# Fewer dense columns, wider gathered rows and another order of picking in a two-tile expert layer

## Chip, cores and metric

One NeuronCore of a Trainium2 chip runs the whole program. The metric is the device time of one launch in microseconds. "PE" is the matrix engine, "DVE" the vector engine, "ACT" the scalar engine, "POOL" the GpSimd engine, "SP" the engine that only issues transfers here.

## What is computed

The program is one encoder block for 256 tokens of 2,048 columns: a combined projection, a gated linear attention, a differential attention, an output projection, and then the part that this change touches, a layer of 16,384 single-neuron experts. Cut to that part, the reference is:

```python
qb = (xb @ w_q).reshape(TB, 8, 2, 128)
s = einsum('thpc,hpnc->thpn', qb, sub_keys)
sv, si = top_k(s, 16)                      # per head: 16 of 128, twice
cand = sv[..., 0, :, None] + sv[..., 1, None, :]
cv, ci = top_k(cand.reshape(..., 256), 16) # 16 experts of 16384
g = softmax(cv)
u, vv = u_tab[eidx], v_tab[eidx]           # rows of 2048 columns
a = gelu(einsum('thkd,td->thk', u, xb))
out = einsum('thk,thkd->td', g * a, vv)
```

Each token has 8 heads of 16 experts, so 128 "slots". A slot needs the dot product of one row of `peer_u` with the token, and later a weighted row of `peer_v`.

## The kernel before

The 256 tokens are two tiles of 128, tile 0 and tile 1. The first expert layer (the dot products) is split by columns of `peer_u`.

**Dense part.** The first `DU = KU*128 = 896` columns are multiplied for all 16,384 experts. A host-side transposed copy `c_uT` comes in as 128 blocks of 128 experts. A block is a tile `ur` (L916, loaded at L917 on SP's queue, `NU = 3` buffers) and seven products per block (L919) with the 256 tokens moving; an f32 product is two instructions in the trace. ACT copies the results (L921) into `Y = [W0, W1]`, two tiles of 64 KB per partition, indexed by expert row and column.

**Gathered part.** The other 1,152 columns are fetched row by row: for each slot `gather_dot` issues an indirect transfer on POOL's queue (L761) of one row for each of 128 tokens into a buffer `g` (`NG = 5` buffers), and DVE forms the dot product with `xb` (L765) into `dots`. There are 128 such gathers for each tile. Before them DVE routes each head (`route`, L731 to L757: top 16 twice, indices, softmax numerator).

**Picking.** When all dense results stand, `pick(tt, t4)` takes those of the chosen experts for four tokens: it loads the row indices broadcast to all partitions (`ib`, L782, three buffers), spreads the column indices by PE (L786), makes a one-hot matrix on ACT (L788, L789), multiplies `Y` with it on PE (L792), selects the row on DVE (L793), sums over partitions on PE (L795) and scales on DVE (L797). There are 32 picks for a tile. `slots_of` (L768 to L777) prepares the indices of a tile, by PE transposes (L773), after its routing.

**Weights.** `weights_of(tt, sT)` adds gathered and dense parts, applies Gelu and the softmax weights, and leaves a row of slot weights in `sT[:, 2]`. `build_w` then writes, four tokens at a time, the weights into a dense expert matrix, W0 for tile 0 and W1 for tile 1: two one-hot matrices (`oj` by POOL, ACT and DVE in turn, `oi` by DVE at L901) and a product (L903). W0 is built in place of tile 0's dense results while tile 1 is picked, and W1 after `weights_of(1)`. Then the second expert layer runs in the same two-part manner (from L985) to the end.

**Order.** The order of instructions on each engine is fixed when the program is built, by a list scheduler with its own estimate of durations: it takes the earliest instruction of the program text that it thinks ready. In the text, all of tile 0's gathers and tile 1's routing come first, then the dense products, then tile 1's gathers with picks and W0 builds between those of heads `H0 = 3` to 7. Each engine runs its instructions in the fixed order, and waits at an instruction whose inputs are not there.

Of the kernel before, what the change touches and what calls it, by code (L numbers as in the profile page):

```python
# [10 lines left out]
F32 = mybir.dt.float32  # L11
# [4 lines left out]
AF = mybir.ActivationFunctionType  # L16
ALU = mybir.AluOpType
# [3 lines left out]
P = 128  # L21
# [19 lines left out]
def block_kernel(ctx: ExitStack, tc: tile.TileContext, A: dict, out: bass.AP):  # L41
    nc = tc.nc
# [11 lines left out]
    bt = pool("bt")  # L54
# [18 lines left out]
    def pa(shape):  # L73
        return paux.tile(list(shape), F32, tag="pa", name="pa")
# [15 lines left out]
    iota = cc[:, 128:256]  # L90
    onec = cc[:, 256:257]
# [61 lines left out]
    for k in range(KT):  # L153
        ps = pa([P, N])
# [488 lines left out]

    KU = 7
    DU = KU * P
    rgt = ExitStack()
    rp = pool("rp", side="right", c=rgt)
# [7 lines left out]

    hgd = rp.tile([P, KU, T], F32, name="hgd")
    hg = [None] * KT
    gf = vrow["g_ffn"]  # L660
    w_o = A["c_w_out"]
    for j in range(8):
# [10 lines left out]
        for b in range(2):  # L673
# [3 lines left out]
            for tt in range(2):  # L677
                nc.tensor.transpose(p2[:, tt * P:(tt + 1) * P], hs[:, tt, k * P:(k + 1) * P], ident)
            hg[k] = hgd[:, k] if k < KU else s2p.tile([P, T], F32, tag=f"s2_{k}", name=f"hg{k}")
            nc.scalar.activation(hg[k], p2, AF.Copy, scale=g)  # L680
# [31 lines left out]
    dots = [gwt[:, tt, 1, :] for tt in range(2)]  # L712
    gsum = [gst[:, tt, :] for tt in range(2)]
    u_tab = A["peer_u"][0]
    NG = 5
    NU = 3
    NI = 3

    def top16(vo, io, src, n):
# [47 lines left out]

    def slots_of(tt):  # L768

        r = bt.tile([P, 3, P], F32, tag=f"b{2 + tt}", name=f"slotT{tt}")  # L770
        ps = pa([P, 2, P])
        for a in range(2):
            nc.tensor.transpose(ps[:, a, :], ij[tt][:, a, :], ident)  # L773
        nc.scalar.activation(r[:, 0:2], ps, AF.Copy)
        nc.scalar.activation(jr[:, tt], ij[tt][:, 1, :], AF.Copy)
        nc.scalar.dma_start(ijd[tt].rearrange("a (b c) -> (a b) c", b=4), ij[tt][:, 0, :])
        return r  # L777

    def pick(tt, t4):

        ib = ep.tile([P, 4, P], F32, tag="ib", name="ib", bufs=NI)
        nc.sync.dma_start(ib.rearrange("p a b -> p (a b)"), ijd[tt][t4:t4 + 1, :].to_broadcast([P, 4 * P]))  # L782
        pj = pa([P, 4, P])
        for q in range(4):
            t = t4 * 4 + q
            nc.tensor.matmul(pj[:, q, :], lhsT=identr[:, t:t + 1].to_broadcast([P, P]), rhs=jr[:, tt], start=True, stop=True)  # L786
        oj = rp.tile([P, 4, P], F32, tag="ohx", name="ojT", bufs=2)
        nc.scalar.activation(oj, pj, AF.Abs, bias=mrow, scale=1.0)  # L788
        nc.scalar.activation(oj, oj, AF.Relu, bias=onec, scale=-1.0)  # L789
        pz = pm([P, 4, P])  # L790
        for q in range(4):
            nc.tensor.matmul(pz[:, q, :], lhsT=Y[tt][:, :, t4 * 4 + q], rhs=oj[:, q, :], start=True, stop=True)  # L792
        nc.vector.scalar_tensor_tensor(ib, ib, prow, pz, op0=ALU.is_equal, op1=ALU.mult)  # L793
        for q in range(4):
            nc.tensor.matmul(pj[:, 0, q:q + 1], lhsT=ib[:, q, :], rhs=onec, start=True, stop=True)  # L795
        ts = slice(t4 * 4, t4 * 4 + 4)
        nc.vector.tensor_mul(dT[:, tt, ts], pj[:, 0, 0:4], rstb[:, tt, ts])  # L797

    def weights_of(tt, sT):

        rc = rp.tile([P, 8], F32, tag="rcs", name="rcs", bufs=2)
        nc.vector.reciprocal(rc, gsum[tt])
        g3 = gw[tt].rearrange("p (h k) -> p h k", k=16)
        nc.vector.tensor_mul(g3, g3, rc.unsqueeze(2).to_broadcast([P, 8, 16]))
        ps = pa([P, 2, P])
        nc.tensor.transpose(ps[:, 0, :], dots[tt], ident)
        nc.tensor.transpose(ps[:, 1, :], gw[tt], ident)
        nc.vector.tensor_add(dT[:, tt], dT[:, tt], ps[:, 0, :])
        nc.scalar.activation(dT[:, tt], dT[:, tt], AF.Gelu)
        nc.vector.tensor_mul(sT[:, 2], dT[:, tt], ps[:, 1, :])  # L810
        ps = pa([P, P])
        nc.tensor.transpose(ps, sT[:, 2], ident)
        nc.scalar.activation(gw[tt], ps, AF.Copy)
# [6 lines left out]
    def queries(h):  # L820
        qt = bt.tile([P, 2, T], F32, tag=f"b{2 + h % 2}", name="pqt")

        def ev_pq(b, ps):
            with tc.high_priority():
                nc.scalar.activation(qt[:, b, :], ps, AF.Copy)
        ps = [pm((P, T)) for _ in range(2)]
        for kh in range(2):
            for k0, raw in load_raw(w_q, h * 256, kh, wait[h][kh]):
                for kk in range(raw.shape[1]):
                    k = k0 + kk  # L830
                    for b in range(2):
                        nc.tensor.matmul(ps[b], lhsT=raw[:, kk, b * P:(b + 1) * P], rhs=hg[k], start=(k == 0), stop=(k == KT - 1))
        for b in range(2):
            ev_pq(b, ps[b])
        with tc.high_priority():
            for tt in range(2):
                ps = pa([P, 2, P])
                for p in range(2):
                    nc.tensor.matmul(ps[:, p, :], lhsT=qt[:, p, tt * P:(tt + 1) * P], rhs=skT[h // 2][:, 2 * (h % 2) + p, :],
                                     start=True, stop=True)  # L840
                s_ = rp.tile([P, 2, P], F32, tag="sS", name="sS", bufs=3)
                nc.scalar.activation(s_, ps, AF.Copy, scale=rst[tt])
                if tt == 0:
                    s0 = s_
            nc.scalar.dma_start(sS1d[h], s_)
            eis[0, h] = route(0, h, s0)
# [14 lines left out]
    rstb = rp.tile([P, 2, P], F32, name="rstb")  # L861
    for tt in range(2):
        ps = pa([P, P])
        nc.tensor.transpose(ps, rst[tt].to_broadcast([P, P]), ident)
        nc.scalar.activation(rstb[:, tt], ps, AF.Copy)
    ijd = [drp.tile([32, 4 * P], F32, name=f"ijd{tt}") for tt in range(2)]
    dT = rp.tile([P, 2, P], F32, name="dT")
    wpc.close()
    ph0.close()
    ph1.close()  # L870
# [4 lines left out]
    W0 = wp01.tile([P, P, P], F32, name="W0")  # L875
# [3 lines left out]
    W1E = "pav"  # L879


    def build_w(oi4, wt, sT, t4):
        ps = pa([P, 4, P])
        for q2 in range(2):
            oj = bt.tile([P, 2, P], F32, tag="ow", name="oj1", bufs=4)
            t = t4 * 4 + q2 * 2
            m = W1E[(t4 * 2 + q2) % len(W1E)]
            if m == "a":
                for q in range(2):
                    nc.scalar.activation(oj[:, q], iota, AF.Abs, bias=sT[:, 1, t + q:t + q + 1], scale=-1.0)  # L890
                nc.scalar.activation(oj, oj, AF.Relu, bias=onec, scale=-1.0)
            elif m == "p":
                for q in range(2):
                    nc.gpsimd.tensor_scalar(oj[:, q], iota, sT[:, 1, t + q:t + q + 1], None, op0=ALU.is_equal)  # L894
            else:
                nc.vector.tensor_tensor(
                    oj, iota.unsqueeze(1).to_broadcast([P, 2, P]), sT[:, 1, t:t + 2].unsqueeze(2).to_broadcast([P, 2, P]),
                    op=ALU.is_equal)
            for q in range(2):
                oi = oi4[:, q2 * 2 + q]  # L900
                nc.vector.tensor_scalar(oi, iota, sT[:, 0, t + q:t + q + 1], sT[:, 2, t + q:t + q + 1], op0=ALU.is_equal,  # L901
                                        op1=ALU.mult)
                nc.tensor.matmul(ps[:, q2 * 2 + q, :], lhsT=oj[:, q], rhs=oi, start=True, stop=True)  # L903
        nc.scalar.activation(wt[:, :, t4 * 4:t4 * 4 + 4], ps.rearrange("p t i -> p i t"), AF.Copy)

    for h in range(8):
        for k in range(16):
            gather_dot(0, h, k, eis[0, h])
        s_ = rp.tile([P, 2, P], F32, tag="sS", name="sS", bufs=3)
        nc.scalar.dma_start(s_, sS1d[h])  # L910
        eis[1, h] = route(1, h, s_)

    for g in range(P // 2):
        ps = pm([P, 2, T])
# [8 lines left out]
    epc = ExitStack()  # L923
    ep = pool("ep2", side="right", c=epc)
    sTs = [slots_of(tt) for tt in range(2)]
    work = [lambda t4=t4: pick(0, t4) for t4 in range(32)] + [lambda: weights_of(0, sTs[0])]
    for t4 in range(32):
        work.append(lambda t4=t4: pick(1, t4))
        work.append(lambda t4=t4: build_w(ep.tile([P, 4, P], F32, tag="oi4", name="oi4", bufs=2), W0, sTs[0], t4))

    H0 = 3
    done, n = 0, len(work)
    for h in range(8):
        for k in range(16):
# [142 lines left out]
def host_vectors(inputs):  # L1077

    r = {"c_vec": np.concatenate([np.asarray(inputs[nm]).reshape(n, P) for nm, n in VEC])}
    w = np.asarray(inputs["w_in"])[0]  # L1080
    r["c_w_in"] = host_blocks(np.concatenate([w[:, :OFF_LR], w[:, OFF_DQ:]], axis=1), 256)
    r["c_w_lr"] = host_blocks(w[:, OFF_LR:OFF_DQ], 32)[0]
    for nm in ("w_branch_gla", "w_branch_diff", "w_out", "peer_w_q"):
        r["c_" + nm] = host_blocks(np.asarray(inputs[nm])[0], 256)

    r["c_uT"] = np.ascontiguousarray(np.asarray(inputs["peer_u"])[0][:, :7 * P].reshape(P, P, 7, P).transpose(0, 3, 2, 1))
    return r


# [50 lines left out]
```

## Time and profile before

| What | Value |
|---|---|
| median of 3 runs | 2665.92 us (2665.3 to 2668.43) |
| profiled execution, its time | 2668.04 us |
| profiled execution, its span | 2666.2 us |
| mean granted PE clock in it | 0.959 of full speed |
| busy PE / DVE / ACT / POOL | 2511.2 / 1937.0 / 1081.0 / 984.3 us |

The span runs from the first to the last instruction of the trace; 1.8 us of the time lie around it. The expert layer's first half lies between about 1187 us (first gather) and 2090 us of the span.

### The profile page before, as it was taken

What the parts mean: (1) busy time and instruction counts of PE and PEld (TensorE: products, weight loads), DVE (VectorE), ACT (ScalarE), POOL (GpSimd) and SP (SyncE); (2) the same over time, 40 slices, a digit from 0 to 9 for tenths busy, and PEclk for the clock granted to TensorE, in tenths of its full rate; (3) what the DMA queues carried; (4) which work ended last, traced back from release to release, by engine and by line L of the source; (5) the groups of instructions that cost most, each with busy time, mean ns of one, the idle gap of its engine ahead of it and who ended that gap; (6) DMA issues with size and microseconds to landing.
All of it is one profiled execution on the core that took longest, in us unless ns stands there. A gap on an engine that the chain in (4) does not pass through costs nothing.

```text
span 2666.2 us, 43563 instructions
## 1 busy us (share of the span) xinstructions
PE 2511.2 (94%) x16631; PEld 2386.3 (90%) x16631; DVE 1937.0 (73%) x3179; ACT 1081.0 (41%) x1948; POOL 984.3 (37%) x999
## 2 busy tenths in 40 slices
PE   8999999999999999999796999989999999999996
PEld 7999999999999999998675777779998889999996
DVE  4778877557777875439997666652357999899998
ACT  4555554345555544421111000013466544444444
POOL 1333310001011001015655655420013777777776
PEclk9999999999999999999898999985699999999998
DMA  4344445554454564579899999971123588888886
GB/s 161 139 155 163 145 171 185 184 188 153 159 169 165 185 225 135 203 267 369 291 372 347 410 408 408 404 267 64 60 68 118 194 303 306 311 317 313 311 309 238
DMA packets 141470, 622.39 MB, mean 233 GB/s; under 512 B 17906, under 2 KB 22828, under 8 KB 116412
## 3 DMA queue, kind: packets, MB, share of 16 engines
q1 hardware_dynamic: 78960, 382.96, 41.2%
q0 software_dynamic: 59216, 230.04, 23.1%
q10 hardware_dynamic: 3084, 6.59, 0.7%
q8 instruction: 131, 2.15, 0.3%
q14 instruction: 79, 0.65, 0.1%
HBM read 613.07 MB, written 5.37 MB: 232 GB/s over the span
## 4 chain that ended last, share of the span: by engine, by line
PE 55%; DVE 15%; issue 13%; POOL 9%; DMA 7%; ACT 0%; POOLq 0%; DVEq 0%; ACTq 0%
PE pm L205 11%; PE pm L203 11%; PE pm L204 11%; POOL g L761 7%; DMA gv<-in_peer_v_dram,ent 5%; PE pm L792 4%; DVE g L765 3%; DVE hs L970 3%; PE pa L795 3%; PE acc L1008 2%; PE pa L903 2%; DMA g<-in_peer_u_dram,ent 1%; PE acc L1009 1%; PE pa L786 1%; DVE vlo L1002 1%
## 5 line engine op out<-in xcount | busy, mean ns | idle before, releaser
L189 DVE TENSOR_TENSOR lo<-raw,hi 128x1024 fp32r<-128x1024 f32 x352 | 451.2, 1283 | 255.6 <-ACT hi L188 253.8
L205 PE MATMUL pm<-hT,lo 128*128 128x256 f32 (+1 forms) x2048 | 579.0, 286 | 7.9 <-DVE lo L189 7.9
L203 PE MATMUL pm<-hT,hi 128*128 128x256 f32 (+1 forms) x2048 | 583.1, 286 | 0.0
L204 PE MATMUL pm<-hT,hi 128*128 128x256 f32 (+1 forms) x2048 | 582.8, 285 | 0.0
L188 ACT ACTIVATE hi<-raw 128x1024 fp32r<-128x1024 f32 x352 | 372.5, 1059 | 333.0 <-PE pm L204 269.7
L765 DVE SCALAR_TENSOR_TENSOR g<-g,xb 128x1152 f32<-128x1152 f32 x256 | 352.9, 1380 | 139.0 <-DMA g<-in_peer_u_dram,ent 137.9
L919 PE MATMUL pm<-hgd,ur 128*128 128x256 f32 x1792 | 408.4, 385 | 34.7 <-DMA ur<-in_c_uT_dram 31.7
L919 PEld LDWEIGHTS pm<-hgd,ur 128*128 128x128 f32 x1792 | 335.6, 191 | 106.5 <-DMA ur<-in_c_uT_dram 30.6
L205 PEld LDWEIGHTS pm<-hT,lo 128*128 128x128 f32 x2048 | 386.2, 190 | 10.7 <-DVE lo L189 9.0
L203 PEld LDWEIGHTS pm<-hT,hi 128*128 128x128 f32 x2048 | 387.5, 189 | 0.4
L204 PEld LDWEIGHTS pm<-hT,hi 128*128 128x128 f32 x2048 | 387.4, 189 | 0.2
L761 POOL DMA_INDIRECT g<-in_peer_u_dram,ent x256 | 289.2, 1130 | 242.9 <-DVE g L765 170.2
L967 POOL DMA_INDIRECT gv<-in_peer_v_dram,ent x256 | 311.9, 1219 | 131.8 <-DVE hs L970 78.4
L1009 PE MATMUL acc<-vhi,wb 128*128 128x368 f32 x1024 | 329.4, 332 | 0.0
L970 DVE SCALAR_TENSOR_TENSOR hs<-gv,gwt,hs 128x576 f32<-128x576 f32 x256 | 285.6, 1115 | 30.8 <-DMA gv<-in_peer_v_dram,ent 26.9
L1009 PEld LDWEIGHTS acc<-vhi,wb 128*128 128x128 f32 x1024 | 191.8, 189 | 0.0
L1008 PE MATMUL acc<-vlo,wwv 128*128 128x368 f32 x512 | 169.3, 341 | 13.3 <-DVE vlo L1000 7.3
L1008 PE MATMUL acc<-vlo,wb 128*128 128x368 f32 x512 | 169.3, 339 | 10.7 <-DVE vlo L1000 4.0
L921 ACT ACTIVATE W<-pm 128x256 f32<-128x256 f32 x128 | 41.9, 380 | 322.8 <-PE pm L919 321.1
L894 POOL TENSOR_SCALAR oj<-cc,slotT 128x128 f32<-128x128 f32 x88 | 59.1, 683 | 253.8 <-PE pa L903 243.3
L792 PE MATMUL pm<-ojT,W 128*128 128x128 f32 x512 | 127.9, 410 | 0.5 <-ACT W L921 0.5
L1008 PEld LDWEIGHTS acc<-vlo,wwv 128*128 128x128 f32 x512 | 95.9, 189 | 24.9 <-DVE vlo L1000 11.3
(882 smaller groups left out, 4669.2 us busy)
## 6 DMA issues: line engine op xcount, KB each, us to landing
raw<-in_c_w_in_dram SPq DMA_DIRECT2D x128, 1024.0 KB
ur<-in_c_uT_dram SPq DMA_DIRECT2D x128, 448.0 KB
raw<-in_c_w_branch_gla_dram SPq DMA_DIRECT2D x16, 1024.0 KB
raw<-in_c_w_out_dram SPq DMA_DIRECT2D x16, 1024.0 KB
raw<-in_c_w_branch_diff_dram SPq DMA_DIRECT2D x16, 1024.0 KB
ib<-ijd SPq DMA_DIRECT2D x64, 256.0 KB
raw<-in_c_peer_w_q_dram SPq DMA_DIRECT2D x13, 1024.0 KB
g<-in_peer_u_dram,ent POOLq DMA_INDIRECT x256
```

Source lines behind the costliest of these rows:

```text
L188: nc.scalar.activation(hi, src, AF.Copy)
L189: nc.vector.tensor_sub(lo, src, hi.bitcast(F32))
L203: nc.tensor.matmul(ps[b], lhsT=wh, rhs=ah, start=(k == 0), stop=False)
L204: nc.tensor.matmul(ps[b], lhsT=wh, rhs=al, start=False, stop=False)
L205: nc.tensor.matmul(ps[b], lhsT=wl, rhs=ah, start=False, stop=(k == KT - 1))
L761: nc.gpsimd.indirect_dma_start(out=g, out_offset=None, in_=u_tab, in_offset=bass.IndirectOffsetOnAxis(ap=ei[:, k:k + 1], axis=0), element_ ...
L765: nc.vector.scalar_tensor_tensor(g, g, 1.0, xb[:, tt, :], op0=ALU.mult, op1=ALU.mult, accum_out=dots[tt][:, s:s + 1])
L919: nc.tensor.matmul(ps[:, b, :], lhsT=ur[:, k, :], rhs=hgd[:, k, :], start=(k == 0), stop=(k == KU - 1))
L967: nc.gpsimd.indirect_dma_start(out=g, out_offset=None, in_=v_tab, in_offset=bass.IndirectOffsetOnAxis(ap=eis[tt, s // 16][:, s % 16:s % 16 ...
L970: nc.vector.scalar_tensor_tensor(hs[:, tt, DC:], g, gw[tt][:, s:s + 1], hs[:, tt, DC:], op0=ALU.mult, op1=ALU.add)
L1008: nc.tensor.matmul(o, lhsT=wh[:, tt, :], rhs=lo[:, ns], start=False, stop=False)
L1009: nc.tensor.matmul(o, lhsT=wl[:, tt, :], rhs=hi[:, ns], start=False, stop=last(tt))
```

## The change

The dense part shrinks from seven to five blocks of 128 columns (640), so a gathered row grows from 1,152 to 1,408 columns. The U blocks get five buffers of 640 columns instead of three of 896, the row buffers are four instead of five, and the score buffers `sS` two instead of three. The sums `dT` of the dense part move into a fourth slice of the tile `slotT`. In the builds of W0 alone, all `oj` are made by POOL, and every second `oi` by three ACT instructions instead of one of DVE. Picks and W0 builds lie among tile 1's heads 2 to 7 instead of 3 to 7.

```diff
-    KU = 7
+    KU = 5
...
-    NG = 5
-    NU = 3
+    NG = 4
+    NU = 5
...
-        r = bt.tile([P, 3, P], F32, tag=f"b{2 + tt}", name=f"slotT{tt}")
+        r = bt.tile([P, 4, P], F32, tag=f"b{2 + tt}", name=f"slotT{tt}")
...
-        nc.vector.tensor_mul(dT[:, tt, ts], pj[:, 0, 0:4], rstb[:, tt, ts])
+        nc.vector.tensor_mul(dTs[tt][:, ts], pj[:, 0, 0:4], rstb[:, tt, ts])
...
-                s_ = rp.tile([P, 2, P], F32, tag="sS", name="sS", bufs=3)
+                s_ = rp.tile([P, 2, P], F32, tag="sS", name="sS", bufs=2)
...
-            m = W1E[(t4 * 2 + q2) % len(W1E)]
+            m = "p" if wt is W0 else W1E[(t4 * 2 + q2) % len(W1E)]
...
-                nc.vector.tensor_scalar(oi, iota, sT[:, 0, t + q:t + q + 1], sT[:, 2, t + q:t + q + 1], op0=ALU.is_equal,
-                                        op1=ALU.mult)
+                if wt is W0 and q:
+                    nc.scalar.activation(oi, iota, AF.Abs, bias=sT[:, 0, t + q:t + q + 1], scale=-1.0)
+                    nc.scalar.activation(oi, oi, AF.Relu, bias=onec, scale=-1.0)
+                    nc.scalar.activation(oi, oi, AF.Copy, scale=sT[:, 2, t + q:t + q + 1])
+                else:
+                    nc.vector.tensor_scalar(oi, iota, sT[:, 0, t + q:t + q + 1], sT[:, 2, t + q:t + q + 1], op0=ALU.is_equal,
+                                            op1=ALU.mult)
...
+    dTs = [r[:, 3] for r in sTs]
...
-    H0 = 3
+    H0 = 2
```

## Rows read from the trace of the kernel before

**Rows 1.** The page's slices of the span: granted PE clock and transfer rate.

```profile
PEclk9999999999999999999898999985699999999998
...
GB/s 161 139 155 163 145 171 185 184 188 153 159 169 165 185 225 135 203 267 369 291 372 347 410 408 408 404 267 64 60 68 118 194 303 306 311 317 313 311 309 238
```

**Rows 2.** Busy us of each engine (instructions) by stage; last clock, DMA share, GB/s.

```profile
core 0: us, PE busy (x) PEld busy (x) DVE busy (x) ACT busy (x) POOL busy (x), PEclk, DMA share, GB/s
...
1187.00:1285.00 98.00, 92.16 (x439) 81.41 (x438) 83.16 (x243) 11.27 (x34) 53.62 (x55) 0.97 0.89 325
1285.00:1418.00 133.00, 97.68 (x434) 81.69 (x433) 128.97 (x401) 15.89 (x59) 83.22 (x85) 0.91 0.93 341
...
1435.00:1762.00 327.00, 300.08 (x1324) 245.18 (x1322) 208.11 (x305) 30.95 (x94) 176.50 (x153) 1.00 1.02 408
1762.00:1778.00 16.00, 8.70 (x39) 8.25 (x38) 11.77 (x19) 3.48 (x6) 5.47 (x5) 0.83 0.75 274
1778.00:1904.00 126.00, 124.60 (x595) 124.54 (x596) 29.94 (x71) 41.30 (x59) 0.00 (x0) 0.53 0.22 67
1904.00:1938.00 34.00, 34.00 (x216) 34.00 (x216) 18.19 (x56) 21.40 (x44) 6.18 (x10) 0.85 0.16 52
1938.00:2037.50 99.50, 98.52 (x682) 98.25 (x681) 52.95 (x155) 60.59 (x118) 20.30 (x34) 0.98 0.19 61
2037.50:2090.00 52.50, 44.08 (x295) 39.51 (x296) 49.78 (x160) 43.73 (x103) 33.46 (x48) 0.92 0.36 127
```

**Rows 3.** The page's costliest groups: the dense products (busy, mean ns | idle before).

```profile
L919 PE MATMUL pm<-hgd,ur 128*128 128x256 f32 x1792 | 408.4, 385 | 34.7 <-DMA ur<-in_c_uT_dram 31.7
```

**Rows 4.** Groups by line and form, 1285 to 1435 us.

```profile
L761 POOL DMA_INDIRECT g<-in_peer_u_dram,ent x60 | 65.5, 1091 | 52.5 <-DVE g L765 14.9 <-DVE tk L723 8.4 <-DVE si L725 7.7
...
L773 PE MATMUL pa<-cc,ijt 128*128 128x128 f32 x4 | 1.4, 442 | 28.7 <-DVE ijt L750 28.7
```

**Rows 5.** Busy time by stage, the dot products (L765) alone; two instructions each.

```profile
1187.00:1418.00 231.00, 122.94 (x172) 0.93 0.91 335
```

**Rows 6.** Groups by line and form, 1435 to 1762 us.

```profile
L765 DVE SCALAR_TENSOR_TENSOR g<-g,xb 128x1152 f32<-128x1152 f32 x153 | 207.8, 1358 | 119.1 <-DMA g<-in_peer_u_dram,ent 118.9
```

**Rows 7.** Timeline of DVE at 1763 us (start us, us).

```profile
1763.88 1.36 DVE L765 SCALAR_TENSOR_TENSOR g<-g,xb 128x1152 f32<-128x1152 f32 x1
...
1765.27 1.36 DVE L765 SCALAR_TENSOR_TENSOR g<-g,xb 128x1152 f32<-128x1152 f32 x1
```

**Rows 8.** Timeline of PE's weight loads, the same build product at two clocks.

```profile
1917.44 1.83 PEld L903 LDWEIGHTS pa<-oi,oj 128*128 128x128 f32 x8
...
1966.90 0.99 PEld L903 LDWEIGHTS pa<-oi,oj 128*128 128x128 f32 x8
```

**Rows 9.** Groups by line, 1762 to 2037.5 us.

```profile
L793 DVE SCALAR_TENSOR_TENSOR ib<-ib,cc,pm 128x512 f32<-128x512 f32 x64 | 47.7, 747 | 94.4 <-PE pm L792 93.0 <-DMA ib<-ijd 1.4
...
L789 ACT ACTIVATE ojT<-ojT,cc 128x512 f32<-128x512 f32 x62 | 44.7, 720 | 1.8
L788 ACT ACTIVATE ojT<-pa,cc 128x512 f32<-128x512 f32 x62 | 42.3, 682 | 94.3 <-PE pa L786 92.1 <-PE pm L792 2.1
L901 DVE TENSOR_SCALAR oi<-cc,slotT 128x128 f32<-128x128 f32 x128 | 38.1, 353 | 12.3 <-PE pa L903 11.0
...
L894 POOL TENSOR_SCALAR oj<-cc,slotT 128x128 f32<-128x128 f32 x44 | 26.5, 613 | 238.0 <-PE pa L903 227.6 <-DVE dT L797 6.3 <-DVE oj L896 4.0
L904 ACT ACTIVATE W<-pa 128x512 f32<-128x512 f32 x32 | 19.0, 592 | 25.0 <-PE pa L903 25.0
L890 ACT ACTIVATE oj<-cc,slotT 128x128 f32<-128x128 f32 x42 | 14.4, 392 | 13.1 <-PE pa L903 13.1
```

**Rows 10.** Timeline at 1325 us: four `oj` of POOL among dot products of DVE.

```profile
1326.63 3.85 POOL L894 TENSOR_SCALAR oj<-cc,slotT 128x128 f32<-128x128 f32 x4
...
1328.10 1.41 DVE L765 SCALAR_TENSOR_TENSOR g<-g,xb 128x1152 f32<-128x1152 f32 x1
```

**Rows 11.** Timeline of POOL at 1763 us: gathers that wait for nothing shown.

```profile
1763.51 1.11 POOL L761 DMA_INDIRECT g<-in_peer_u_dram,ent  x1 [0.30 <-issue]
```

More of the change, by code (lines that the diff above doesn't have):

```diff
@@ L807, in weights_of @@
         nc.tensor.transpose(ps[:, 1, :], gw[tt], ident)
-        nc.vector.tensor_add(dT[:, tt], dT[:, tt], ps[:, 0, :])
-        nc.scalar.activation(dT[:, tt], dT[:, tt], AF.Gelu)
-        nc.vector.tensor_mul(sT[:, 2], dT[:, tt], ps[:, 1, :])
+        nc.vector.tensor_add(dTs[tt], dTs[tt], ps[:, 0, :])
+        nc.scalar.activation(dTs[tt], dTs[tt], AF.Gelu)
+        nc.vector.tensor_mul(sT[:, 2], dTs[tt], ps[:, 1, :])
         ps = pa([P, P])
@@ L866, in block_kernel @@
     ijd = [drp.tile([32, 4 * P], F32, name=f"ijd{tt}") for tt in range(2)]
-    dT = rp.tile([P, 2, P], F32, name="dT")
     wpc.close()
@@ L908, in block_kernel @@
             gather_dot(0, h, k, eis[0, h])
-        s_ = rp.tile([P, 2, P], F32, tag="sS", name="sS", bufs=3)
+        s_ = rp.tile([P, 2, P], F32, tag="sS", name="sS", bufs=2)
         nc.scalar.dma_start(s_, sS1d[h])
@@ L1084, in host_vectors @@
         r["c_" + nm] = host_blocks(np.asarray(inputs[nm])[0], 256)
-    r["c_uT"] = np.ascontiguousarray(np.asarray(inputs["peer_u"])[0][:, :7 * P].reshape(P, P, 7, P).transpose(0, 3, 2, 1))
+    r["c_uT"] = np.ascontiguousarray(np.asarray(inputs["peer_u"])[0][:, :5 * P].reshape(P, P, 5, P).transpose(0, 3, 2, 1))
     return r
```

## The prediction

> **What bounds the kernel now.** I read the page's slices first [rows 1]: the transfer rate stands at its highest, 404 to 410 GB/s, in four slices of the expert layer's first half and drops to 60 to 70 right behind them, where the granted clock also falls. So this half has two stages of opposite kind. The stage table [rows 2] gives their edges.
>
> From 1187 to 1285 us PE works on the queries (92 of 98 us) while the first gathers start. From 1285 to 1762 us it does the dense products. Up to 1418 DVE is the bound (128.97 of 133 us busy: routing and dot products together). From 1435 the transfers are: 408 GB/s, DMA share 1.02, with PE close behind (300 of 327 us). The gathers of both tiles end about when the dense products do, at 1778 against 1762 us.
>
> [...] From 2037.5 on (W1, second layer) the change touches nothing, so I carry those 628.7 us over.
>
> The question is how much earlier than 2037.5 us the last tile 1 pick ends.
>
> **The dense stage, now 477 us (1285 to 1762).** 1,792 product instructions are busy 408.4 us, 0.228 each; PE's idle time before them has 31.7 us of waits for U blocks [rows 3]. Another 28.7 us go to the index transposes of `slots_of`, which stand in PE's fixed order among the products and wait for DVE's routing [rows 4]. The remaining 8 us are mostly waits on ACT's copies.
>
> Five products a block make 1,280 instructions: 1,280 x 0.228 = 292 us, 117 less.
>
> Waits for U blocks: a block takes 327 / (1,324/14) = 3.46 us now, against 14 x 0.228 = 3.19 of work, and a gather 327 / 153 = 2.14 us [rows 2, 6]. The rows are 1,152 x 4 x 128 = 590 KB and the blocks 459 KB, so 276 and 133 GB/s. After, a block is 328 KB and wants 2.28 us, 144 GB/s; that leaves 264 of the 408 for rows of 721 KB, one in 2.73 us. Bytes in flight stay about the same: four rows of 721 KB are 2.88 MB against five of 590 KB, 2.95, and five blocks 1.64 MB against three, 1.38. So U should get no smaller share; I take 16 us, between nothing and the present 31.7.
>
> Waits for routing: 86 dot products lie before 1418 us [rows 5], each longer. Back to back one takes 1.39 us [rows 7]; in proportion to its columns 1.39 x 1408/1152 = 1.70. That delays the routing by up to 86 x 0.31 = 27 us, while PE comes to the same place in the order with fewer microseconds of products behind it; the builder's order, though, will put the transposes further back. So 28.7 to 56 us; I take 34, near the present row, since both sides of the wait move.
>
> Sum: 292 + 16 + 34 + 8 = 350, so the dense stage ends at 1635 instead of 1762, 127 us earlier (bounds: 292 + 0 + 29 + 8 = 329 and 292 + 32 + 56 + 8 = 388, that is 148 and 89 us earlier).
>
> The queries before it I leave at their time: they are PE work, and 36 wider rows in that stretch would add 36 x 131 KB / 408 GB/s = 12 us of transfers at most, my bound. Two score buffers instead of three add waits on ACT in the same stretch and during routing; these lie behind ACT's waits for routing and behind the four result banks that PE can fill ahead, at the latter 10 us. `dT`'s move is the same DVE work in another tile: nothing.
>
> **The pick stage, now 275.5 us (1762 to 2037.5).** What was free there no longer is. At 1635 us about 92 dot products of the stretch up to 1441 and (1635 - 1441)/2.73 = 71 more are done, some 160 of 256. So 96 gathers with their dot products now lie among 32 picks, 32 pairs and the weights, about one per item.
>
> Hand-over, 1762 to 1778: DVE's fixed order holds the first picks behind late dot products. I keep its 16 us.
>
> Tile 0's picks: 126 us, 595 PE instructions, 20 to a pick, so 4.23 us each. DVE needs 1.70 for a dot product and 0.75 + 0.16 for a pick [rows 9], 2.6 us; transfers need 721 + 262 KB (`ib` is 2 KB on 128 partitions), 2.4 us at 408 GB/s. PE at the low clock remains the bound, and nothing in the change adds to its stream: 126 us. At a full clock a pick would cost 133.5/32 - 0.99 = 3.18 us [rows 2, 8], 102 us in all, my lower bound.
>
> The pairs: now 133.5/32 = 4.17 us. After, a pair of items comes with two gathers. Per pair
> - DVE: 2 x 1.70 + 0.91 + two `oi` at 0.35 = 5.0 us (the other two `oi` and its share of `oj` have left);
> - ACT: 0.68 + 0.72 + 0.59 for copies and one-hots, and six new instructions at 0.39, 4.3 us;
> - POOL: two gathers at 1.09 and 0.30 of issue each [rows 4, 11], and four `oj`. They cost 0.61 each alone [rows 9], but 3.85 us for four beside dot products, 0.97 each [rows 10]: 2.78 + 3.88 = 6.7 us;
> - PE: 4.17 us at full clock, and 4.23 + 1.83 = 6.1 at half [rows 8], which it may fall to when it waits for the others.
>
> [...]
>
> I take 6.2 us, between PE at half clock and POOL, since POOL is free during tile 0's picks and part of the 64 gathers can go ahead there: 32 x 6.2 = 198 us, 65 more than now. Bounds: 133 (all gathers hidden) and 213 (6.7).
>
> Sum: 16 + 126 + 198 = 340 against 275.5, 65 us longer (bounds 251 and 355: 24 shorter, 80 longer). The tile 1 picks end at 1635 + 340 = 1975 instead of 2037.5.
>
> **Total.** Made against the profiled execution's own 2668.0: 2668.0 - 127 + 65 = 2606. That execution lies 2.1 us above the median of the runs, so I forecast 2604 us. The bounds together give 2495 to 2680.
>
> **Rivals.**
> 1. *The gathers hide wholly.* If POOL and DVE use the slack of tile 0's picks and the clock holds, a pair is DVE's 5.0 us and a pick 3.2: 16 + 102 + 160 = 278, so 2668 - 127 + 2 = 2543. For it: 0.98 from 1938 on. Against: 0.53 for 126 us in a stream that never paused.
> [...]
> 3. *U blocks do not come faster.* Gathers outrun them, a block still takes 3.46 us: 443 + 34 + 8 = 485 us, the stage ends at 1770; nearly all gathers are done by then, and the pick stage stays 275: 2676. For it: transfers are full at 1435 to 1762. Against: bytes in flight, above. [...]
>
> **Chances.** The forecast's own case (2570 to 2640) 0.62; rival 1 (2520 to 2570) 0.22; rival 2 0.09, of which 0.03 ends within 0.2%; rival 3 0.06; elsewhere 0.01. A measurement tells 0.2%, 5 us, from no change. So faster 0.85, same 0.04, slower 0.11. To leave out no more than 2 in 10 I take the forecast's case and the nearer part of rivals 1 and 2: 2530 to 2655.
>
> **What would show it.** Dense products x1280 at 0.228, ending near 1635 us; gathers every 2.7 us beside them; a clock near 0.5 in tile 0's picks; POOL over 90% busy or waiting for DVE in the pairs, pitch about 6.2 us; tile 1's last `dT` near 1975; 628 us from there to the end. Wrong would be a dense stage beyond 1675 us (routing or U waits), or pairs near 4.5 or above 8 us.

## The result, and the profile after

| | before | after |
|---|---|---|
| median of 4 runs | 2667.18 us (2665.3 to 2668.61) | 2629.91 us (2623.52 to 2634.61) |
| ratio, 95% interval | | 0.9859 [0.9835, 0.9883] |
| profiled execution, its span | 2668.04, 2666.2 us | 2627.45, 2625.4 us |
| mean granted PE clock in it | 0.959 | 0.94 |

The change gains 1.4%, 37 us. The prediction was 2604 us, a gain of 62, so the direction holds and the size is 26 us off. A few source lines have moved: the dense products are now L923 (were L919), their copies L925, POOL's `oj` L893, DVE's `oi` L905, ACT's new `oi` L901 to L903, the build product L907.

The stage table of after, in the columns of [rows 2]: busy us of each engine (instructions), then granted clock, DMA share and GB/s.

```profile
core 0: us, PE busy (x) PEld busy (x) DVE busy (x) ACT busy (x) POOL busy (x), PEclk, DMA share, GB/s
1187.00:1285.00 98.00, 94.36 (x453) 83.22 (x452) 84.37 (x233) 11.91 (x36) 49.69 (x49) 0.98 0.88 327
1285.00:1422.00 137.00, 107.88 (x484) 92.56 (x483) 125.53 (x377) 22.57 (x78) 78.85 (x79) 0.90 0.90 326
1422.00:1594.00 172.00, 163.67 (x696) 126.96 (x695) 107.11 (x131) 22.66 (x69) 64.98 (x66) 1.00 1.02 409
1594.00:1621.00 27.00, 26.59 (x120) 22.35 (x120) 0.70 (x2) 3.67 (x12) 0.94 (x1) 1.00 0.54 196
1621.00:1740.00 119.00, 115.17 (x619) 113.14 (x617) 88.26 (x143) 44.97 (x67) 51.16 (x40) 0.70 0.88 302
1740.00:1918.50 178.50, 160.08 (x908) 155.60 (x907) 121.95 (x227) 115.37 (x290) 165.21 (x166) 0.76 0.71 232
1918.50:1999.50 81.00, 0.01 (x1) 0.04 (x1) 54.52 (x69) 0.07 (x1) 49.86 (x35) 0.50 0.85 289
1999.50:2052.00 52.50, 44.13 (x289) 38.65 (x290) 49.84 (x159) 42.85 (x101) 33.43 (x47) 0.92 0.35 127
```

The edges are the last dense product (1621), the end of tile 0's picks (1740), tile 1's last pick (1918.5), and tile 1's last dot product (1999.5). The row to look at is the seventh: for 81 us PE has nothing to do. Before, the last pick and the start of W1 fell together; now they lie 81 us apart. The page's slices, in answer to [rows 1], show the same hole as a 5 in the clock (the thirtieth slice, 1903 to 1969 us), while 273 GB/s still flow:

```profile
PEclk9999999999999999999998999677757999999998
...
GB/s 161 144 145 170 153 146 195 191 180 163 164 161 162 174 228 161 183 244 356 326 328 324 408 408 258 322 288 237 227 273 229 204 302 307 323 317 316 311 310 243
```

**The dense products**, from the page's costliest groups, in answer to [rows 3]: 1,280 at 0.232 us, with 6.7 us of waits for U blocks where there were 31.7.

```profile
L923 PE MATMUL pm<-hgd,ur 128*128 128x256 f32 x1280 | 296.8, 387 | 12.9 <-DMA ur<-in_c_uT_dram 6.7
```

And from the groups by line and form, 1270 to 1435 us, the transposes of [rows 4], which waited 28.7 us:

```profile
L773 PE MATMUL pa<-cc,ijt 128*128 128x128 f32 x4 | 1.4, 446 | 24.9 <-DVE ijt L750 24.9
```

So 296.8 + 12.9 + 24.9 + 1.4 = 336 us, 1285 to 1621.

**The dot products** of L765 alone by stage (two instructions to one), as in [rows 5]:

```profile
core 0: us, DVE busy (x), PEclk, DMA share, GB/s
1285.00:1422.00 137.00, 67.66 (x80) 0.90 0.90 326
1422.00:1594.00 172.00, 107.11 (x131) 1.00 1.02 409
1594.00:1621.00 27.00, 0.70 (x2) 1.00 0.54 196
1621.00:1740.00 119.00, 64.36 (x81) 0.70 0.88 302
1740.00:1918.50 178.50, 78.32 (x94) 0.76 0.71 232
1918.50:1999.50 81.00, 53.96 (x66) 0.50 0.85 289
```

Beside the dense products one comes every 172/65.5 = 2.6 us. Then they stop for 27 us. 40 come among tile 0's picks, 47 in the pairs of a tile 1 pick and a W0 build, and 33 are left when the last pick is done. The stop in the timelines of DVE, POOL and PE at 1593 us (start us, us, engine, line, and in brackets the idle time before with what ended it):

```profile
1593.07 1.63 DVE L765 SCALAR_TENSOR_TENSOR g<-g,xb 128x1408 f32<-128x1408 f32 x1 [0.92 <-DMA g<-in_peer_u_dram,ent]
...
1624.74 1.52 DVE L793 SCALAR_TENSOR_TENSOR ib<-ib,cc,pm 128x512 f32<-128x512 f32 x2 [30.04 <-DMA ib<-ijd]
1626.19 1.62 DVE L765 SCALAR_TENSOR_TENSOR g<-g,xb 128x1408 f32<-128x1408 f32 x1
```

```profile
1594.98 0.94 POOL L761 DMA_INDIRECT g<-in_peer_u_dram,ent  x1 [1.62 <-DVE g L765]
1628.08 0.94 POOL L761 DMA_INDIRECT g<-in_peer_u_dram,ent  x1 [32.17 <-DVE g L765]
```

```profile
1621.71 7.33 PE L792 MATMUL pm<-ojT,W 128*128 128x128 f32 x32 [0.47 <-ACT W L925]
```

DVE's fixed order puts the first pick's selection (L793) behind 136 dot products (31 begun before 1285 us, then 39, and 66 beside the dense products). DVE got there at 1594.7, while PE had 27 us of dense products before it, and the pick's product (L792) starts only at 1621.71. The releaser named is the load of `ib`, but the first pick's products had ended only just before (the ACT instruction that they release, L788, starts at 1623.77), so the load can have cost about 1 us of the 30.04. All four row buffers are full behind the waiting instruction, so POOL issues no gather for 32.17 us.

**In the pairs**, groups by line and form from 1740 to 1918.5 us:

```profile
L893 POOL TENSOR_SCALAR oj<-cc,slotT 128x128 f32<-128x128 f32 x122 | 110.2, 914 | 1.4
L765 DVE SCALAR_TENSOR_TENSOR g<-g,xb 128x1408 f32<-128x1408 f32 x47 | 78.0, 1659 | 28.8 <-DMA g<-in_peer_u_dram,ent 28.8
...
L761 POOL DMA_INDIRECT g<-in_peer_u_dram,ent x44 | 55.6, 1263 | 12.2 <-issue 6.0 <-DVE slotT L797 2.6 <-DVE slotT L810 1.8
```

POOL is busy 165.21 of 178.5 us, 110.2 of them with `oj` at 0.914 each, and issues 44 gathers in 32 pairs. How many dot products stand ahead of a pick is part of DVE's fixed order: in the trace 222 come before the last pick's selection and 34 behind it, and no faster gather would alter that.

**Behind the last pick**, the same groups from 1918.5 to 1999.5 us:

```profile
L765 DVE SCALAR_TENSOR_TENSOR g<-g,xb 128x1408 f32<-128x1408 f32 x33 | 53.7, 1627 | 26.3 <-DMA g<-in_peer_u_dram,ent 25.5
L761 POOL DMA_INDIRECT g<-in_peer_u_dram,ent x32 | 48.1, 1504 | 23.6 <-DVE g L765 17.8 <-issue 5.7 <-DVE wb L986 0.2
...
L806 PE MATMUL pa<-cc,gwt 128*128 128x128 f32 x1 | 0.4, 446 | 81.6 <-DVE g L765 81.6
```

L806 is the transpose of `dots` in `weights_of(1)`. It waits 81.6 us for the 33 dot products of this stretch, 81/33 = 2.45 us each. The chain of waits there says it too:

```profile
1990.58 7.03 DMA g<-in_peer_u_dram,ent
...
1997.71 1.64 DVE g L765 x2
...
1999.49 0.45 PE pa L806
```

### The profile page after: what moved, and what is told of

Its sections match the earlier page's. It is cut to its first block, busy times and chain, and to the rows that moved or that the text cites. A ratio compares the mean times of both kernels' runs of the same rounds, so it can differ in the third digit from the quotient of the medians.

```text
span 2625.4 us, 42612 instructions
## 1 busy us (share of the span) xinstructions
PE 2410.2 (92%) x16119; PEld 2295.2 (87%) x16119; DVE 1975.4 (75%) x3094; ACT 1111.9 (42%) x2077; POOL 1088.5 (41%) x1083
## 5 line engine op out<-in xcount | busy, mean ns | idle before, releaser
L189 DVE TENSOR_TENSOR lo<-raw,hi 128x1024 fp32r<-128x1024 f32 x352 | 451.7, 1285 | 257.3 <-ACT hi L188 253.8
L765 DVE SCALAR_TENSOR_TENSOR g<-g,xb 128x1408 f32<-128x1408 f32 x256 | 420.1, 1644 | 134.6 <-DMA g<-in_peer_u_dram,ent 133.7
L761 POOL DMA_INDIRECT g<-in_peer_u_dram,ent x256 | 299.8, 1171 | 331.0 <-DVE g L765 232.6
L923 PE MATMUL pm<-hgd,ur 128*128 128x256 f32 x1280 | 296.8, 387 | 12.9 <-DMA ur<-in_c_uT_dram 6.7
L923 PEld LDWEIGHTS pm<-hgd,ur 128*128 128x128 f32 x1280 | 239.9, 192 | 68.5 <-issue 17.6
L893 POOL TENSOR_SCALAR oj<-cc,slotT 128x128 f32<-128x128 f32 x172 | 148.9, 877 | 18.7 <-PE pa L907 13.9
L925 ACT ACTIVATE W<-pm 128x256 f32<-128x256 f32 x128 | 41.6, 380 | 204.2 <-PE pm L923 187.4
L792 PE MATMUL pm<-ojT,W 128*128 128x128 f32 x512 | 124.7, 409 | 1.1 <-ACT ojT L789 0.6
```

The source lines that it names most:

```text
L189: nc.vector.tensor_sub(lo, src, hi.bitcast(F32))
L761: nc.gpsimd.indirect_dma_start(out=g, out_offset=None, in_=u_tab, in_offset=bass.IndirectOffsetOnAxis(ap=ei[:, k:k + 1], axis=0), element_ ...
L765: nc.vector.scalar_tensor_tensor(g, g, 1.0, xb[:, tt, :], op0=ALU.mult, op1=ALU.mult, accum_out=dots[tt][:, s:s + 1])
L923: nc.tensor.matmul(ps[:, b, :], lhsT=ur[:, k, :], rhs=hgd[:, k, :], start=(k == 0), stop=(k == KU - 1))
```

## The experiments

Each ratio is to the kernel before on the same chip; differences between versions are differences of these ratios (0.01 is 26.7 us).

**Theory.** The gain is cut not by the picks but by a second queue that ends later than they do: the gathers with their dot products. It loses about 27 to 32 us in the stop ahead of the first pick, and it is starved in the pairs because all `oj` of W0 now stand on POOL between the gathers. **Rivals.** R1: the gathers are held by their row buffers (four, of 721 KB), whatever stands on POOL. R2: the moved builds help, and undoing them makes the pairs as much longer as the tail gets shorter.

**The builds of W0 as before, the rest as after.**

```diff
-            m = "p" if wt is W0 else W1E[(t4 * 2 + q2) % len(W1E)]
+            m = W1E[(t4 * 2 + q2) % len(W1E)]
...
-                if wt is W0 and q:
...
-                else:
-                    nc.vector.tensor_scalar(oi, iota, sT[:, 0, t + q:t + q + 1], sT[:, 2, t + q:t + q + 1], op0=ALU.is_equal,
-                                            op1=ALU.mult)
+                nc.vector.tensor_scalar(oi, iota, sT[:, 0, t + q:t + q + 1], sT[:, 2, t + q:t + q + 1], op0=ALU.is_equal,
+                                        op1=ALU.mult)
```

> The change with W0's builds as before (one-hots by POOL, ACT and DVE in turn, all `oi` by DVE). Theory A (the last dot product sets the end, and POOL's one-hots hold up the gathers among the pairs): the gathers among the pairs come every 2.7 us instead of 3.8, only some 11 dot products stand behind the last pick instead of 34, the last one ends 40 to 50 us earlier, time 2580 to 2595. Theory B (four row buffers and the transfers set the pace of the gathers, POOL's queue does not): the last dot product stays near 1999 us, time 2625 to 2635.

2600.16 us, 0.9765 [0.9745, 0.9785]: in ratio 0.0094, 25 us, better than the whole change. The stage row of the pairs and the wait at L806 (window 1900 to 1980 us):

```profile
1740.00:1945.00 205.00, 179.69 (x923) 174.74 (x921) 178.66 (x360) 86.98 (x163) 145.53 (x115) 0.66 0.84 287
```

```profile
L806 PE MATMUL pa<-cc,gwt 128*128 128x128 f32 x1 | 0.4, 444 | 24.1 <-DVE g L765 24.1
```

71 dot products now lie in the pairs instead of 47. The pairs take 205 us instead of 178.5, with PE (179.69, at a granted clock of 0.66) and DVE (178.66) the fullest engines, and the tail falls from 81 to 24. So both the theory and R2's trade are there, 57 us against 26.5; the theory's part is the larger. The time lies above the 2580 to 2595 expected.

What this run leaves open: it takes `oj` off POOL and `oi` off ACT at once, and it changes the builder's order with them. On DVE 245 dot products now come before the last pick, where the whole change has 222. That POOL's queue by itself holds the gathers up is argued from its 165.21 busy us of 178.5, not shown apart from that order.

**Before, with the new builds and `H0 = 2` alone.** The same edit the other way round in the kernel before.

> The kernel before with the new W0 builds and H0 = 2, all widths and buffers as before. Theory A: no gathers are left among the pairs, POOL needs 4 x 0.61 = 2.4 us of a pair of 4.17, so nothing moves: 2660 to 2672. Rival (the new builds lengthen a pair by themselves, through POOL's one-hots that PE waits for): pairs of 5 us or more, time 2690 or more.

2678.74 us, 1.0052 [1.0032, 1.0072]: a miss: some 14 us slower, where no change was expected. The stage rows:

```profile
1285.00:1768.00 483.00, 409.48 (x1794) 336.93 (x1792) 348.48 (x712) 49.27 (x158) 269.26 (x248) 0.95 0.98 379
1768.00:1910.00 142.00, 129.98 (x604) 129.60 (x604) 37.38 (x75) 45.39 (x67) 3.86 (x4) 0.52 0.25 81
1910.00:2049.00 139.00, 136.34 (x924) 135.51 (x922) 50.87 (x134) 113.28 (x290) 73.83 (x124) 0.96 0.21 62
```

The pairs take 139 us against 133.5 [rows 2]; the dense stage ends 6 us later, and tile 0's picks take the same 142 as the two rows of before. In the dense stage POOL makes eight `oj` in one stretch of 8.0 us during tile 1's routing, and the index transposes wait 39.3 us instead of 28.7 [rows 4]. That the one makes the other was not tested. PE is busy 136.34 of the pairs' 139 us, so what the new builds take off DVE shortens nothing there.

**The whole change, with dot products ahead of tile 0's picks.** Only a rule for DVE's order is added: pick `t4` of tile 0 has to stand behind dot product 20 + 5*t4/4 of tile 1; the builder arranges the rest around it. No semaphore is added, both are DVE's own (`sels` and `dot_ins` hold the instructions of L793 and L765).

```diff
+    for tt, t4, sel in sels:
+        k = 20 + 5 * t4 // 4 if tt == 0 else -1
+        if k >= 0:
+            tc.add_manual_dep(sel.ins, dot_ins[1, k].ins.name, mybir.DependencyInfo(mybir.DependencyClass.NoSync, mybir.DependencyReason.DATA), reason="order")
     weights_of(1, sTs[1])
```

> The change, with the fixed order of DVE altered: pick j of tile 0 stands behind dot product 20 + 1.25 j of tile 1, so that gathers go on until the dense products end. Theory A: the stop of 30 us in the gathers ahead of the first pick vanishes, 12 or more dot products move there, 16 instead of 34 stand behind the last pick, time 2595 to 2612. Theory B: the transfers only move, the last dot product stays near 1999 us, time 2625 to 2635.

2597.57 us, 0.9751 [0.9732, 0.9769], 29 us better in ratio than the whole change. The stop is gone: 374 GB/s over the whole dense stage, where the whole change moved 358. The dot products by stage and the wait of the same transpose (here L810, window 1900 to 1980 us):

```profile
1285.00:1621.00 336.00, 192.43 (x233) 0.95 0.97 374
...
1929.00:1966.00 37.00, 25.76 (x32) 0.54 0.81 284
```

```profile
L810 PE MATMUL pa<-cc,gwt 128*128 128x128 f32 x1 | 0.4, 445 | 36.2 <-DVE g L768 36.2
```

116 instead of 106 dot products in the dense stage, 16 instead of 33 in the tail. The last pick is 10.5 us later (1929); what makes it later was not tested.

**Both together.** The first and the third edit.

> The change with both: W0's builds as before, and tile 0's picks held behind dot products 20 + 1.25 j of tile 1. Theory A: no dot product is left behind the last pick, which itself moves little (it came at 1945 to 1952 us with the builds undone), so the end is set by picks and pairs: 2575 to 2590, less than the sum of the two single gains (30 and 32 us) because both shorten the same tail. If the two gains were independent: 2568.

2568.89 us, 0.9646 [0.962, 0.9671]: 57 us better in ratio, where the two alone give 25 + 29 = 54. They add up within the noise, where less than their sum was expected: two separate causes. This is the fastest version here, 3.5% ahead of before. Its pairs:

```profile
1750.00:1943.50 193.50, 174.18 (x910) 169.70 (x910) 166.22 (x345) 85.74 (x162) 121.02 (x105) 0.66 0.80 274
```

All 256 dot products stand before the last pick, the transpose of `dots` waits for none of them, and the last pick (1943.5) sets the end: what the prediction had taken for granted is true here, not in the change itself.

**Two heads less.** 32 of tile 1's dot products (heads 6 and 7) with their gathers are left out and set to zero, so this is the time of less work; a mark in the second layer that waited for dot product 100 waits for 90.

```diff
+    nc.vector.memset(dots[1][:, 96:128], 0.0)
...
-            gather_dot(1, h, k, eis[1, h])
+            if h < 6:
+                gather_dot(1, h, k, eis[1, h])
...
-    HD = 100
+    HD = 90
```

> The change without the gathers and dot products of tile 1's heads 6 and 7, whose dot products are set to zero; the order of everything else is the same. Theory A: with 32 of the 34 last dot products gone, weights of tile 1 follow the last pick at once and the time falls by the tail, 70 to 80 us, to 2550 to 2560. Theory C (the matrix engine at its low clock or the row transfers set the end in any case): the time falls by less than 30 us.

2558.51 us, 0.9599 [0.9582, 0.9616]: 69 us. Up to the last pick nothing moves (1921.5 against 1918.5):

```profile
1740.00:1921.50 181.50, 165.06 (x905) 160.27 (x905) 122.45 (x228) 115.67 (x290) 167.41 (x167) 0.73 0.72 227
```

So the tail of the whole change is these dot products and nothing else. The last part, W1 onward, begins 76 us earlier (1923.5 against 1999.5) and is 9 us longer than in the whole change, which leaves 67 in the profiled executions.

**Three row buffers instead of four** (`NG = 3`, the rest as after), for R1.

> The change with three row buffers instead of four. If the row buffers set the pace of the gathers (latency over buffers), a gather beside the dense products takes 2.55 x 4/3 = 3.4 us at most and one in the lone tail 3.2 instead of 2.4, and the last dot product comes 60 to 110 us later: 2690 to 2740. If the transfers or POOL set it, less than 15 us: below 2645.

2695.44 us, 1.0127 [1.0103, 1.0151], slower than before. The last pick is earlier (1892), the tail 175 us:

```profile
1892.00:2067.00 175.00, 0.45 (x3) 0.31 (x3) 103.91 (x129) 0.40 (x1) 80.86 (x64) 0.50 0.77 259
```

64 dot products at 2.73 us, where four buffers give 2.45. So the buffers have a part in the pace when nothing else runs, but not the whole of it: a pace set by them alone would be 2.45 x 4/3 = 3.3 us, an estimate that leaves a row's time in flight as it is. Most of the longer tail is order again, with 192 dot products before the last pick instead of 222. R1 holds in part, beside the theory and not in place of it, since the builds and the order alone took the whole tail away with four buffers. Five buffers of this size were not tried.

**Six blocks dense, the builds as before** (`KU = 6`, `NU = 4`, `NG = 4`, host copy of six blocks).

> Six blocks of 128 columns dense (768 columns, rows of 1,280), four U buffers, W0's builds as before, the rest as the change. Theory A: dense products end 58 us later (256 instructions at 0.228), near 1680; gathers are done before the last picks, so the end is the pick stage behind the dense products, 275 to 300 us: last pick at 1955 to 1980, time 2583 to 2610. If the gathers still set the end there is again a wait of tens of us at the last weights.

2581.55 us, 0.9702 [0.9674, 0.973]. The pairs:

```profile
1775.00:1950.00 175.00, 158.37 (x912) 155.14 (x912) 137.69 (x314) 84.73 (x162) 92.86 (x88) 0.77 0.65 222
```

Dense products end at 1652, the last pick at 1950, and no wait for gathers is left: all 256 dot products stand before the last pick. The dense stage is 31 us longer than in the whole change, where 58 was expected: from 1400 us on 1,092 products are busy 238.4 us, 0.218 each, and wait 0.5 us for U blocks, where the whole change from there on has 197.9/840 = 0.236 and 6.5 us. Without any edit of the order it beats the whole change by 1.6%, but not the fastest version above.

**`H0 = 3` instead of 2**, the rest as after.

> The change with H0 = 3, so picks stand among tile 1's heads 3 to 7 in the text. The order of picks and dot products on DVE comes out the same, since the builder takes what it thinks ready; both theories: no difference from the change, 2625 to 2635.

2633.5 us, 0.989 [0.9865, 0.9916]: no difference to the whole change that is clear of the noise. In both traces the dot products and the picks' selections follow each other on DVE in the same order, 136 before the first pick and 222 before the last, so where the program text begins to interleave the picks doesn't decide where the builder puts them.

## Why the prediction was half right

**The dense stage: right, and better than forecast.** It ended at 1621, forecast 1635. Products took 296.8 us (292), U blocks' waits 6.7 (16), transposes 24.9 (34, and less than the lower bound of 28.7), the other waits 12.9 - 6.7 = 6.2 (8). Rival 3 is out. In the stretch to 1594 a block takes 172/69.6 = 2.47 us, 133 GB/s or 32% of 409, where the sum had 2.28 us. In the kernel before it was 133 of 408 GB/s, 33%, on three U buffers. PE was not content with 2.47 us: in the run with three row buffers 815 products from 1400 us on are busy 178.9 us, 0.220 each and 2.20 us a block, and wait 0.2 us for U blocks, at 344 GB/s over that dense stage against 358 in the whole change, where they take 0.236 each from there on. So part of the 296.8 us that count as busy came with the fuller transfers.

**Tile 0's picks: over-sized.** 119 us, forecast 16 + 126 = 142. The hand-over was a term too many: PE went from the last dense product to the first pick in 0.5 us. And the granted clock was 0.70 where the forecast kept that of before, 0.53 [rows 2].

**The pairs: the right engine, and luck in the size.** 178.5 us, 5.58 each, forecast 6.2. POOL is the fullest engine as worked out (165.21 of 178.5), `oj` cost 0.914 (0.97 foreseen). But it wasn't 64 gathers that POOL carried there, only 44. An estimate from these rows, 64 gathers at 1.263 + 0.30 and 122 `oj` at 0.914, would fill POOL for 212 us, 6.6 a pair; the pairs were shorter because 20 gathers were left for later. `oj` beside dot products took as long as [rows 10] had it, and no longer. PE, for which the forecast had 6.1 us a pair at half clock, was granted 0.76 (0.66 at the lowest in any run) and was busy 160.08 of 178.5 us, 5.0 a pair. The slower side, to which the chances give 0.09 as rival 2, begins at 8.1 us a pair, (275.5 + 127 - 142)/32, where the change would gain nothing; no run shows such a pair, 205/32 = 6.4 is the longest (builds undone), so it is out.

**The step that failed** is the premise "the question is how much earlier than 2037.5 us the last tile 1 pick ends", together with "96 gathers ... about one per item". The last pick came at 1918.5, 56.5 us before the 1975 forecast (14 from the dense stage, 23 from tile 0's picks, 19.5 from the pairs). But the gathers were by then not done: 33 of the 256 dot products were left, 81 us with PE idle. 81 - 56.5 = 24.5 us is what W1's start was late against the forecast; W1 and the second layer took 626 us (628.7), which leaves about the 21.5 us between 2606 and 2627.45. That the time came within 1% of the forecast is luck in part: picks that were 56.5 us early hid most of a wait of 81 us that the sum didn't have.

Three things made the queue late. Not 160 but 136 dot products were done when the first pick started. Some 14 of the 24 were missing at 1441 us already: the sum carried 92 over from the old kernel, whose rows are narrower, and 78 were begun by then. Most of the rest is the stop: DVE's order, fixed from estimates, had the pick in front of the next ones, and DVE stood 30 us before it (run with the dot products ahead: 29 us). And among the pairs, with 122 `oj` on POOL, there were 44 gathers; I had priced 64 as a longer pair, but the builder had put the rest behind the last pick (run with the builds undone: 25 us). The prediction counted these gathers into the items and never asked where the last of them ends if the order lets picks and builds pass them.

Rival 1 came nearer on the picks' time (278 us against 119 + 178.5 = 297.5; the forecast had 340), but not by its reason: the clock was 0.70 and 0.76, and the gathers were not hidden but left behind. The prediction's own bounds were added wrongly at the upper end: 2668 - 89 + 80 is 2659, not 2680.

Open: why the clock in tile 0's picks was 0.70 and not 0.53 (in the run with two heads less it was 0.65 from 1621 to 1740, with PE busy 115.65 of 119 us); why W1 and the second layer take 9 us longer with two heads less; and how the 14 us of the builds alone in the old kernel divide, beyond the 6 and 5.5 us that the stages show, and why the dense stage is longer in it.

## What to carry to other kernels

When several streams must all be done before the next stage, follow each to its own end and take the latest; the one that bounds the old kernel may not bound the new one. When a change shortens what stands beside a stream of transfers, ask where the transfers that were hidden there go, and which engine issues them: work moved onto that engine can cost them time there (25 us here, together with the order that it changed), and a program whose order is fixed when it is built may put them behind everything else. An order fixed from estimates stopped DVE here for 30 us in front of an instruction whose input was late, with all that stood behind it; letting ready work go first there was worth 29 us without removing an instruction.

## What the runs showed of the hardware beside this

- Gathers alone, with four buffers of 721 KB, moved 289 GB/s at a DMA share of 0.85 (1918.5 to 1999.5 us), with three 259 at 0.77 (1892 to 2067 us of that run); with U blocks beside them the same four brought the total to 409 at 1.02 (1422 to 1594 us).
- POOL's gather instruction took 0.94 us where it followed a wait and DVE's dot product was just done, and 1.50 us on average in the tail, where dot products fill 53.96 of DVE's 81 us.
- PE's granted clock: 0.50 in the 81 us in which it idled, 0.70 in tile 0's picks with PE busy 115.17 of 119 us, 0.53 before with 124.6 of 126 [rows 2]. In windows of 4 us it was 0.50 in 12 of 29 and 1.00 in 3 in the picks after (1621 to 1737), and 0.50 in 28 of 31 before (1778 to 1902). In the fastest version it was 0.59 with 126.45 of 131. What sets it within the same stream of picks these rows don't show.
